# Two transformer blocks on one core: the tile scheduler orders the program by its timeline simulation instead of its default machine

## The chip, the cores and the metric

The kernel runs on one core of one Trainium2 chip. The metric is device time in microseconds of one execution, the median of several. The engines of the core are TensorE (PE; its weight loads have a row of their own, PEld), VectorE (DVE), ScalarE (ACT), GpSimd (POOL) and SyncE (SP), whose queue issues the DMA transfers.

## What is computed

The reference runs two blocks one after the other on 512 tokens of width 1024, all in float32:

```python
x = first_block(x, c, ctx, c_ctx, ...)      # 2 layers, modulated by c and c_ctx
return second_block(x, even_w_in_2, ...)    # 2 layers, each a mixer and a feed-forward
```

The first block normalises and modulates the tokens and 256 context tokens. Its layer 0 is windowed attention with 16 query heads, 4 key heads and a sink; the tokens also read all context keys. Its layer 1 is latent attention (16 heads, keys of 64 + 32) over context and tokens. Each layer ends with a gated output projection that is added to the tokens, and the block with a norm.

The second block has an even layer, in which 8 attention heads stand beside 4 heads of a linear recurrence (HGRN2, in blocks of 32 tokens), and an odd layer with 16 heads of chunked attention and a table of relative biases. After each mixer follow a norm, a residual sum, and a feed-forward of width 2816 with a convolution of three taps over the tokens, a GELU gate and a projection back.

## The kernel before, in words

**Arithmetic.** Large products are made of three TensorE products of fp32r halves: a weight tile is split into a high part H and a low part L, the activations too, and H·H, H·L and L·H are summed in PSUM (`gemm_T`, `oproj_chunk`). `mm` (L293) records every product, so nearly all matmuls carry its line, and `act` (L290) every ScalarE operation. `wchunk` (L295) brings one weight tile: a DMA into `raw` (L300), a ScalarE copy to H and a VectorE subtraction for L (L304). There are two or three buffers of `raw` and three of H and L.

**Stages, in the order of the trace.** Modulation and the turning of x (until about 100 us); attention of layer 0 (`attn_a`, until about 410); its output projection, gates and norms (`out_proj`, until about 500); the latent projections and gates of layer 1 and its attention (`attn_b`, until about 810); the output projection; the even mixer (`even`, about 880 to 1060); its output projection and norm (`mixer_end`); the feed-forward (`ffn`, until about 1470); the odd mixer (`odd`, until about 1700), `mixer_end` and the second feed-forward.

**Order in the program.** The kernel is written with Python generators. In attention `merge` and `mix` take turns between the scores of one head, the values of the head before, and filling work: the projections for coming heads (`g_qk`, `g_q`, `g_v`, `g_g`). `skew` makes the transposes of a block of P run two or three blocks ahead of the products that use them. Q and K of a pair of heads are gathered by DMA copies (`dcopy`, L591) from the projected tiles. There are 8 pairs in `attn_a`, 8 in `attn_b`, 4 in `even` and 8 in `odd`. In `out_proj` each row block's projection is followed by its residual sum and norm: `row_r` (L352, VectorE), `rstd` (L336, GpSimd, a power of -0.5), the product x·rstd (L365 or L367, VectorE, tile xhat), and then the transposes on TensorE (L375), which `turn` records some chunks of the next block's projection later. In `attn_b` the same is done with L1157 for the latent projections. In the recurrence of `even` (`g_h`) the tile U is made by TensorE and ScalarE, run through 14 dependent VectorE operations (L1556), used in products (po from U and hq), normalised, and transposed (L1582).

**What sets the order on the engines.** All operations are recorded inside one `TileContext`. When it is left, its scheduler runs the recorded program against a model of the machine: whenever an engine of the model can take an instruction, it is given the one of highest priority among those whose operands and buffers are ready in the model. Priority is the order of recording, shifted at L329 and L1738 by `high_priority(50)`; at L1567 `issue_after` ties the order of some products by hand. The sequence that each engine received in the model is the sequence of its queue on the chip, where each queue runs in order and waits by semaphores. The DMA queue of SyncE is ordered in the same way. The model before is the scheduler's default one.

## Time and profile before

| | |
|---|---|
| time, median of 3 runs | 2116.98 us (2109.93 to 2120.24) |
| profiled execution, its own time | 2119.62 us |
| its span, first to last instruction | 2117.8 us |
| instructions in the span | 28799, of which 10609 matmuls and as many weight loads |
| mean granted TensorE clock | 0.988 of full speed |
| moved by DMA | 223.65 MB, mean 106 GB/s |

Busy time of an engine is the time in which it has an instruction under way. Matmuls are pipelined, so the records of two of them overlap. "Idle before" is the time for which an engine stood still ahead of an instruction; the name behind the arrow is what ended it. [...]

### The profile page before, as it was taken

What the parts mean: (1) busy time and instruction counts of PE and PEld (TensorE: products, weight loads), DVE (VectorE), ACT (ScalarE), POOL (GpSimd) and SP (SyncE); (2) the same over time, 40 slices, a digit from 0 to 9 for tenths busy, and PEclk for the clock granted to TensorE, in tenths of its full rate; (3) what the DMA queues carried; (4) which work ended last, traced back from release to release, by engine and by line L of the source; (5) the groups of instructions that cost most, each with busy time, mean ns of one, the idle gap of its engine ahead of it and who ended that gap; (6) DMA issues with size and microseconds to landing.
All of it is one profiled execution on the core that took longest, in us unless ns stands there. A gap on an engine that the chain in (4) does not pass through costs nothing.

```text
span 2117.8 us, 28799 instructions
## 1 busy us (share of the span) xinstructions
PE 2032.1 (96%) x10609; PEld 1688.5 (80%) x10609; DVE 1293.2 (61%) x2491; ACT 1056.4 (50%) x2044; POOL 74.0 (3%) x162
## 2 busy tenths in 40 slices
PE   7899999998999999998999999999999999999998
PEld 4788888778788887876778888887888878888886
DVE  5588788846478886657756444423566775444323
ACT  5477677725367763555534333322466754333321
POOL 2100000000000000000000000000000000000000
PEclk9999999999999999999999999999999999999999
DMA  7344423322444332232223233232565533333332
GB/s 261 100 132 135 115 85 97 118 71 69 124 94 109 86 97 80 94 90 61 60 90 114 96 100 100 91 99 80 138 158 152 140 120 100 100 100 94 96 96 83
DMA packets 80893, 223.65 MB, mean 106 GB/s; under 512 B 13408, under 2 KB 19312, under 8 KB 80752
## 3 DMA queue, kind: packets, MB, share of 16 engines
q1 hardware_dynamic: 80752, 221.81, 34.8%
q8 instruction: 84, 1.38, 0.3%
q14 instruction: 57, 0.47, 0.1%
HBM read 176.67 MB, written 4.19 MB: 85 GB/s over the span
## 4 chain that ended last, share of the span: by engine, by line
PE 82%; DVE 7%; ACT 5%; issue 2%; DMA 2%; POOL 2%; SPq 0%; POOLq 0%; ACTq 0%; DVEq 0%
PE pj L293 33%; PE S L293 28%; PE po L293 13%; PE tp L293 2%; DVE wL L304 2%; PE tp L1305 2%; PE tp L1100 1%; ACT wH L290 1%; POOL rstd L336 1%; ACT tmp L290 1%; ACT junk L290 1%; DVE XL L584 1%; PE tp L375 1%; PE tp L1792 1%; ACT P L290 1%
## 5 line engine op out<-in xcount | busy, mean ns | idle before, releaser
L304 DVE TENSOR_TENSOR wL<-raw,wH 128x1024 fp32r<-128x1024 f32 (+2 forms) x291 | 354.1, 1221 | 465.4 <-ACT wH L290 453.2
L290 ACT ACTIVATE wH<-raw 128x1024 fp32r<-128x1024 f32 (+2 forms) x291 | 305.5, 1053 | 546.4 <-PE S L293 217.6
L293 PE MATMUL pj<-XH,wH 128*128 128x512 f32 (+1 forms) x672 | 259.9, 390 | 2.9 <-ACT tmp L290 1.5
L293 PE MATMUL pj<-XL,wH 128*128 128x512 f32 (+1 forms) x672 | 258.9, 389 | 0.1
L293 PE MATMUL pj<-XH,wL 128*128 128x512 f32 (+1 forms) x672 | 256.0, 384 | 0.5 <-DVE wL L304 0.5
L293 PE MATMUL S<-K,Q 96*128 96x384 f32 (+4 forms) x864 | 189.2, 329 | 3.9 <-ACT P L290 3.0
L293 PE MATMUL S<-XH,wH 128*128 128x512 f32 (+1 forms) x456 | 170.0, 373 | 1.0 <-ACT wH L290 1.0
L293 PE MATMUL S<-XH,wL 128*128 128x512 f32 (+1 forms) x456 | 170.1, 373 | 0.5 <-DVE wL L304 0.5
L293 PE MATMUL S<-XL,wH 128*128 128x512 f32 (+1 forms) x456 | 169.9, 373 | 0.0
L293 PEld LDWEIGHTS S<-K,Q 128*128 128x128 f32 (+1 forms) x864 | 140.7, 189 | 19.2 <-ACT P L290 7.3
L293 PEld LDWEIGHTS pj<-XH,wH 128*128 128x128 f32 x672 | 127.4, 190 | 28.5 <-ACT tmp L290 2.3
L293 PEld LDWEIGHTS pj<-XH,wL 128*128 128x128 f32 x672 | 127.0, 190 | 22.4 <-DVE wL L304 0.8
L293 PEld LDWEIGHTS pj<-XL,wH 128*128 128x128 f32 x672 | 127.1, 190 | 22.0 <-issue 0.4
L290 ACT ACTIVATE PTH<-tp 128x512 fp32r<-128x512 f32 (+2 forms) x192 | 91.3, 480 | 45.1 <-PE tp L1100 14.0
L584 DVE TENSOR_TENSOR PTL<-tp,PTH 128x512 fp32r<-128x512 f32 (+2 forms) x192 | 103.6, 543 | 10.2 <-ACT PTH L290 9.5
L293 PEld LDWEIGHTS S<-XH,wH 128*128 128x128 f32 x456 | 86.2, 189 | 16.6 <-ACT wH L290 1.7
L293 PEld LDWEIGHTS S<-XH,wL 128*128 128x128 f32 x456 | 86.2, 189 | 15.7 <-DVE wL L304 1.0
L293 PEld LDWEIGHTS S<-XL,wH 128*128 128x128 f32 x456 | 86.2, 189 | 15.2
L290 ACT ACTIVATE XH<-tp 128x512 fp32r<-128x512 f32 x128 | 75.1, 596 | 43.4 <-PE tp L375 24.0
L584 DVE TENSOR_TENSOR XL<-tp,XH 128x512 fp32r<-128x512 f32 x128 | 86.9, 686 | 10.6 <-ACT XH L290 9.5
L290 ACT ACTIVATE P<-S,nm 128x768 f32<-128x768 f32 (+1 forms) x96 | 72.5, 757 | 31.5 <-DVE nm L1018 12.4
L293 PE MATMUL po<-PTH,V 128*128 128x256 f32 (+1 forms) x224 | 78.8, 355 | 2.7 <-ACT PTH L290 2.3
(482 smaller groups left out, 4500.8 us busy)
## 6 DMA issues: line engine op xcount, KB each, us to landing
raw<-in_up SPq DMA_DIRECT2D x88, 512.0 KB, 3.5
raw<-in_ada SPq DMA_DIRECT2D x48, 512.0 KB, 4.2
raw<-in_dn SPq DMA_DIRECT2D x44, 512.0 KB, 3.5
raw<-in_o_o SPq DMA_DIRECT2D x11, 512.0 KB, 4.3
x<-in_x SPq DMA_DIRECT2D x8, 512.0 KB, 9.0
raw<-in_a_q SPq DMA_DIRECT2D x8, 512.0 KB, 4.7
raw<-in_a_g SPq DMA_DIRECT2D x8, 512.0 KB, 3.7
raw<-in_a_o SPq DMA_DIRECT2D x8, 512.0 KB, 3.6
```

Of the source, the lines that this page charges most:

```text
L290: self.nc.scalar.activation(out, in_, func, **kw)
L293: return self.nc.tensor.matmul(out, l, r, start=start, stop=stop, **kw)
L304: nc.vector.tensor_sub(L[:, :n], raw[:, :n], H[:, :n].bitcast(F32))
L336: self.nc.gpsimd.tensor_tensor(r, ms, self.c_mh[:, :n], op=ALU.pow)
L375: nc.tensor.transpose(tp[:, kk, :], xh[g][:, kk * P:(kk + 1) * P], self.ident)
L584: self.nc.vector.tensor_sub(L, src, H.bitcast(F32))
L1100: nc.tensor.transpose(tp[:, (i - i0) * P:(i - i0 + 1) * P], Ps[i][0][:, at(i) * P:(at(i) + 1) * P], self.ident)
L1305: nc.tensor.transpose(tp[:, i * P:(i + 1) * P], Ps[i][:, kb * P:(kb + 1) * P], self.ident)
L1792: nc.tensor.transpose(tp[:, (i - kb) * P:(i - kb + 1) * P], Ps[i][0][:, kb * P:(kb + 1) * P], self.ident)
```

## The change

The context is built with one more argument, by which its scheduler runs the program against its timeline simulation, a second model of the same machine with other durations and queues, in place of the default one. The recorded operations, their priorities, the buffers and the edges of `issue_after` are the same. Of the model's result only the order of each engine's queue, the order of the DMA queue and the choice among a tag's buffers go into the program.

```diff
-    with tile.TileContext(nc) as tc:
+    with tile.TileContext(nc, schedule_with_timeline_sim=True) as tc:
         Prog(tc, I, out).build()
```

## Rows read from the trace of the kernel before

**Rows 1.** The page, busy us, share of the span and instructions.
```profile
PE 2032.1 (96%) x10609; PEld 1688.5 (80%) x10609; DVE 1293.2 (61%) x2491; ACT 1056.4 (50%) x2044; POOL 74.0 (3%) x162
```
**Rows 2.** The page, the chain that ended last, by engine.
```profile
PE 82%; DVE 7%; ACT 5%; issue 2%; DMA 2%; POOL 2%; SPq 0%; POOLq 0%; ACTq 0%; DVEq 0%
```
**Rows 3.** Busy time by stretch; its first line says the columns.
```profile
core 0: us, PE busy (x) PEld busy (x) DVE busy (x) ACT busy (x) POOL busy (x), PEclk, DMA share, GB/s
0.00:100.00 100.00, 79.49 (x400) 60.37 (x401) 55.58 (x109) 46.25 (x95) 22.94 (x33) 0.95 0.56 187
100.00:400.00 300.00, 295.63 (x1778) 254.74 (x1776) 249.16 (x605) 219.61 (x465) 14.03 (x58) 1.00 0.35 103
400.00:600.00 200.00, 186.32 (x869) 153.93 (x870) 120.56 (x238) 89.33 (x191) 7.19 (x12) 0.95 0.34 107
600.00:800.00 200.00, 195.15 (x1157) 164.25 (x1156) 171.66 (x264) 139.50 (x277) 0.00 (x0) 1.00 0.37 96
...
900.00:1100.00 200.00, 181.81 (x1082) 146.01 (x1082) 125.75 (x287) 103.98 (x234) 4.60 (x5) 0.97 0.26 80
...
1150.00:1470.00 320.00, 320.00 (x1400) 262.75 (x1399) 133.62 (x154) 105.09 (x133) 0.15 (x1) 1.00 0.31 99
...
1530.00:1680.00 150.00, 147.06 (x875) 127.27 (x873) 104.46 (x325) 98.77 (x233) 2.32 (x12) 0.99 0.58 151
...
1790.00:2110.00 320.00, 320.00 (x1399) 262.44 (x1398) 128.05 (x150) 99.10 (x126) 1.65 (x3) 1.00 0.29 94
```
**Rows 4.** The chain in order of time, feed-forward: start us, us, what.
```profile
1187.81 5.44 PE pj L293 x24
```
**Rows 5.** TensorE by line and shape: count, busy us, mean ns, idle before.
```profile
L375 PE MATMUL tp<-ident,xhat 128*128 128x128 f32 x176 | 27.5, 287 | 13.6 <-DVE xhat L365 11.2 <-DVE modv L389 2.3
...
L293 PE MATMUL S<-i,kn 32*128 32x128 f32 x128 | 10.9, 285 | 3.6 <-ACT U L290 3.3 <-ACT kn L290 0.3
...
L1582 PE MATMUL tp<-ident,tmp 128*128 128x128 f32 x16 | 5.1, 327 | 5.6 <-DVE tmp L1577 5.6
...
L293 PE MATMUL po<-U,hq 128*32 128x128 f32 x120 | 4.3, 276 | 2.6 <-DVE U L1556 2.6
...
L1157 PE MATMUL tp<-ident,xhc 128*128 128x128 f32 x14 | 3.4, 292 | 3.2 <-DVE xhc L1144 2.0 <-DVE ss L1139 1.2
```
**Rows 6.** Timeline of TensorE, 838 to 848: start us, us, instruction, idle before.
```profile
838.66 0.39 PE L293 MATMUL pj<-wH,oH 128*128 128x512 f32 x1
840.13 0.66 PE L375 MATMUL tp<-ident,xhat 128*128 128x128 f32 x4 [1.08 <-DVE xhat L365]
840.54 0.48 PE L293 MATMUL pj<-wL,oH 128*128 128x512 f32 x1
```
**Rows 7.** Timeline of TensorE in the recurrence, 948 to 975.
```profile
956.35 0.39 PE L293 MATMUL pj<-XH,wL 128*128 128x512 f32 x1
959.32 1.07 PE L293 MATMUL po<-U,hq 128*32 128x128 f32 x30 [2.58 <-DVE U L1556]
963.32 0.47 PE L1582 MATMUL tp<-ident,tmp 128*128 128x128 f32 x1 [2.92 <-DVE tmp L1577]
```
**Rows 8.** Waits of SyncE's queue: us in total, times, longest us.
```profile
SPq L300 <- DVE wL L304: 1003.4, 199, 21.3
```
**Rows 9.** The page, the costliest group: all weight splits on VectorE.
```profile
L304 DVE TENSOR_TENSOR wL<-raw,wH 128x1024 fp32r<-128x1024 f32 (+2 forms) x291 | 354.1, 1221 | 465.4 <-ACT wH L290 453.2
```
**Rows 10.** Timeline of SyncE's queue in the odd mixer: the last copies of two pairs.
```profile
1585.20 1.24 SPq L591 DMA_DIRECT2D K<-tL  x2
...
1683.40 1.25 SPq L591 DMA_DIRECT2D K<-tL  x2
```
**Rows 11.** DMA issues: count, KB each, median us from issue to landing.
```profile
K<-tL SPq DMA_DIRECT2D x32, 128.0 KB, 2.3
```
**Rows 12.** Timeline of TensorE in the odd mixer: first scores of two heads.
```profile
1594.88 0.34 PE L293 MATMUL S<-K,Q 128*128 128x128 f32 x2
...
1687.97 0.30 PE L293 MATMUL S<-K,Q 128*128 128x128 f32 x1 [0.24 <-DMA K<-tL]
```

## The prediction

> **What bounds the kernel now.** I read the page's busy line first, then the chain of work that ended last, then the busy time by stretch, and last what the matmul queue waits for. TensorE is busy 2032.1 of 2117.8 us; VectorE stands at 61% and ScalarE at 50% [rows 1], and the chain runs through matmuls for 82% of its length [rows 2]. So the kernel is bound by the matmul queue, and a new order of the same instructions can only take from, or add to, the 85.7 us in which that queue stands idle, plus what the clock loses with it.
>
> The table by stretch says where those 85.7 us lie [rows 3]. The two feed-forward parts (1150 to 1470 and 1790 to 2110) are full to the last digit: 320.00 of 320. There the chain shows 24 matmuls in 5.44 us, one every 0.227 us [rows 4]. No order makes these 640 us shorter. The attention parts are nearly full: 4.4 us idle of 300 (100 to 400), 4.9 of 200 (600 to 800), 2.9 of 150 (1530 to 1680). The idle time sits elsewhere: 20.5 us in the first 100, 13.7 in 400 to 600 (end of the first mixer, start of the second), 18.2 in 900 to 1100 (the even mixer with its recurrence). In these three the granted clock is below one as well: 0.95, 0.95 and 0.97.
>
> **Part 1: transposes that stand too early in the queue.** The change alters no instruction, only the estimate by which the scheduler decides when an operand will be ready, and so who comes first on each engine. The trace shows where the present estimate is wrong. On TensorE 13.6 us are spent before the transposes of the normalised rows (L375) and 3.2 us before those of L1157; the recurrence adds 5.6 us (L1582), 2.6 (the product with U) and 3.6 (the product that makes U) [rows 5]. Sum: 28.6 us, a third of all idle time. One case in full [rows 6]: the output projection runs until 838.66, the queue then waits 1.08 us for VectorE's xhat, does four transposes at 840.13, and goes on with the very same projection at 840.54 (pj from wL and oH). The trace gives that projection no wait of its own; it only stood behind. The scheduler thought the chain VectorE, GpSimd, VectorE to be over about 1.1 us sooner than it is. An order that puts five projection matmuls (5 x 0.227 = 1.13 us) ahead of the transposes loses nothing.
>
> What is late next: ScalarE and VectorE split the transposed rows 1.1 us later, which matters only for the last row block of a stage, behind which there is no projection left. With four to six blocks per stage I count one in four of these waits as staying. The term is (13.6 + 3.2) x 3/4 = 12.6 us, its bounds 0 (the new estimate is as wrong as the old one) and 16.8.
>
> For the recurrence the case is less clean. At 956.35 the last ready matmul goes out, the product with U waits 2.58 us, the next transposes 2.92 us [rows 7], and only then a projection of 24 matmuls starts. If that projection's weights were there, it could have filled both holes; whether they were, the trace does not say. I take half of 5.6 + 2.6 + 3.6 = 11.8, which is 5.9 us; bounds 0 and 11.8.
>
> **Part 2: new holes in the attention parts.** These stages hold their two chains (scores of one head, values of the one before) closely interleaved, and another estimate will cut them elsewhere. The trace of before has no row for it, so I bound it: below zero by nothing, since their idle share is already the smallest outside the feed-forward; above by the worst stretch with the same kind of work, 900 to 1100, idle 9.1%. I take the poorest attention stretch, 600 to 800 (2.4% idle), for all of them: 300 us x 2.4% is 7.3 instead of 4.4, and 150 us x 2.4% is 3.7 instead of 2.9, together +3.7 us. At 9.1% the three stretches (650 us, 12.2 us idle now) would cost +47 us.
>
> **Part 3: the feed-forward parts, the start and the end.** Cost nothing. In the feed-forward, what hides a changed order is the prefetch of weights: VectorE is busy 133.6 us of 320 and ScalarE 105.1 [rows 3], so a weight tile split somewhat later still arrives in time. If that cover went, each of the two parts would pay for the missing weight tile in its first matmuls only. The first 100 us (granted clock 0.95, 20.5 us idle) and the last 8 us are chains that begin with the first load and end with the last store, with no other work at hand; I leave them as they are.
>
> [...]
>
> **The sum.** 12.6 + 5.9 - 3.7 = 14.8 us less. The profiled execution took 2119.62 us (span 2117.8 and 1.8 around it), 2.64 above the median of 2116.98; 2119.62 - 14.8 - 2.64 gives 2102 us, 0.7% faster.
>
> **The rivals.** *Nothing nets out (same).* The new order moves some waits later and makes others earlier. For it: the holes are spread over dozens of places, and what Part 1 gives is eaten by Part 2 as soon as the attention parts go from 2.4% to about 4.5% idle (650 us x 4.5% = 29 against 12.2). Against it: the waits in rows 5 are all of one sign. To this belongs the case that the switch changes hardly anything, because both estimates rank the ready instructions alike. Time: 2117 us.
>
> *Head copies behind weight loads (slower).* All transfers go out from SyncE's one queue in order, and this queue already stands 1003.4 us behind weight loads that wait for a buffer to come free, 199 times, 5.04 us each, 21.3 at most [rows 8]. There are 291 weight tiles [rows 9], so 68% of them wait. The copies that make Q and K of a pair of heads share this queue. If the new estimate puts a weight load ahead of a pair's copies, they go out 5.04 us later. What they can bear differs: for one pair the last copy is issued at 1585.20 and takes 1.24 us for two issues [rows 10], lands 2.3 us later [rows 11], and scores follow at 1594.88 [rows 12], a lead of 6.1 us; for another the last is issued at 1683.40 [rows 10], and the scores at 1687.97 already wait 0.24 us for it [rows 12]: no lead. At a mean lead of 3.1 us each hit costs 1.9 us; 28 pairs (8 + 8 + 4 + 8) x 0.68 x 1.9 = 36 us: 2153 us. It decides from the point where a load waits longer than the lead. For it: the copies have no slack in at least one place. Against it: in the trace of before nearly nothing on TensorE waits for them.
>
> *A much larger gain.* The order could let TensorE overlap weight loading and streaming better everywhere. In rows, the weight loads are busy 80% [rows 1], at best 254.74 of 300 us [rows 3]; all of the kernel at that share would take 1688.5 / 0.849 = 1989 us. Against it: in the feed-forward the share is only 262.75 of 320, 82%, and yet there is no idle time, so the share follows the width of the matmuls and not the order. [...]
>
> **How the numbers follow.** The forecast, waits shortened by more than new ones are made, has 0.43; the large gain 0.02; so faster by over 0.5% (about what a measurement of this kernel can tell from no change, 10.6 us) has 0.45. Nothing nets out: 0.25. Slower, by the copies or by attention parts at up to 9.1% idle (2117 + 47 = 2164): 0.30. The low end is the gain's far bound: 28.6 us of waits and 16 of clock off the median give 2072; I go to 2068. The high end, 2158, takes in the copies' 2153 and most of the way to 2164. The forecast's own range is 2072 to 2106.
>
> **What would show it.** In the profile after: the same counts, 10609 matmuls and 291 weight tiles; the idle time before L375 down from 13.6 to some 5 us, and projection matmuls standing before the transposes at the end of each stage; the stretch of the recurrence less than 18 us idle; both feed-forward parts still 320 of 320, each only begun earlier. If the waits at L375 are as long as before, Part 1 is wrong. If TensorE waits for DMA into K or Q, the copies were the thing. If attention stretches show over 4.5% idle, Part 2 was too small.

## The result and the profile after

The changed kernel takes 2187.11 us (median of four runs, 2185.10 to 2195.54), the kernel before 2118.05 on the same chip: ratio 1.0341, interval 1.0301 to 1.0381. It is slower by 69 us, where 15 us less were forecast, and it lies above the range that the prediction gave. The profiled execution has a span of 2193.7 us, 75.9 more than before, at a mean granted clock of 0.968 instead of 0.988.

The page's busy line of the changed kernel, to be held against [rows 1]:

```profile
PE 2054.3 (94%) x10609; PEld 1716.4 (78%) x10609; DVE 1288.9 (59%) x2491; ACT 1057.5 (48%) x2046; POOL 77.0 (4%) x162
```

The counts are the same, 10609 matmuls. TensorE's idle time rose from 85.7 to 139.4 us (+53.7) and its busy time by 22.2 us, though it does the same work. The second figure goes with the granted clock: in the second feed-forward part, at 1.00 in both kernels, 1399 matmuls take 320.00 us in each. Busy time by stretch says where both lie. The columns are those of [rows 3]; the bounds are the beginning and end of a part in this trace, or two points up to which TensorE has run the same matmuls in both kernels:

```profile
84.00:439.00 355.00, 325.03 (x1914) 279.98 (x1913) 267.11 (x649) 236.63 (x497) 15.89 (x58) 0.96 0.33 96
504.60:573.90 69.30, 68.08 (x377) 60.57 (x375) 49.27 (x120) 40.55 (x98) 5.39 (x9) 1.00 0.36 120
626.30:806.90 180.60, 172.29 (x1023) 146.47 (x1024) 153.57 (x236) 122.42 (x245) 0.00 (x0) 1.00 0.36 89
940.90:1118.70 177.80, 140.40 (x846) 114.31 (x845) 102.18 (x255) 81.74 (x202) 4.04 (x4) 0.84 0.18 54
1210.00:1530.00 320.00, 320.00 (x1401) 262.75 (x1400) 130.22 (x149) 102.88 (x128) 0.00 (x0) 1.00 0.29 97
1593.00:1784.00 191.00, 181.84 (x1047) 158.16 (x1046) 130.47 (x405) 120.82 (x287) 2.03 (x14) 0.97 0.54 142
1865.00:2185.00 320.00, 320.00 (x1399) 262.41 (x1398) 128.37 (x151) 99.25 (x126) 1.65 (x3) 1.00 0.28 94
```

The same stretches of the kernel before. The counts of matmuls agree within two, but for the odd mixer, the last line, which has 27 fewer here:

```profile
89.00:410.00 321.00, 315.54 (x1913) 272.19 (x1912) 266.79 (x648) 234.39 (x496) 14.03 (x58) 1.00 0.35 101
480.20:560.60 80.40, 73.91 (x375) 64.57 (x373) 48.83 (x120) 38.93 (x94) 5.30 (x9) 0.94 0.31 103
606.70:782.90 176.20, 172.71 (x1024) 146.36 (x1022) 152.67 (x237) 123.56 (x246) 0.00 (x0) 1.00 0.39 101
916.00:1057.50 141.50, 126.80 (x845) 102.11 (x845) 100.40 (x257) 83.52 (x203) 4.04 (x4) 0.95 0.23 68
1527.00:1703.00 176.00, 172.42 (x1020) 147.50 (x1018) 127.01 (x401) 117.77 (x281) 2.61 (x14) 0.99 0.56 147
```

The first attention part lasts 34 us longer: its idle time went from 5.5 to 30.0 us, and its busy time rose by 9.5 at a clock of 0.96 instead of 1.00. The even mixer lasts 36 us longer: 37.4 us idle instead of 14.7, and 13.6 more busy at a clock of 0.84 instead of 0.95. The odd mixer is 15 us longer (3.6 to 9.2 us idle). The second attention part loses 4 us (3.5 to 8.3 us idle). One stretch gained: the end of the first output projection with the latent projections behind it (the second line) takes 69.3 us instead of 80.4, with 1.2 us idle instead of 6.5 and a clock of 1.00 instead of 0.94. At the points with the same matmuls behind them, the changed kernel is late by 29.3 us after the first attention part, by 13.3 after that gain, by 23.9 at the end of the second attention part, by 25.0 at the start of the even mixer's line and 61.2 at its end, by 63.6 through the first feed-forward and by 75.6 through the second. The feed-forward parts are what they were, 320.00 of 320.

Which waits these are, TensorE's table of waits tells (waited for, us in total, times, longest):

```profile
PE po L293 <- DVE U L1556: 13.7, 4, 6.0
PE tp L375 <- DVE xhat L365: 7.4, 3, 3.8
PE S L293 <- DMA Q<-tL: 7.3, 4, 3.1
PE tp L1100 <- DVE PTL L584: 7.1, 10, 1.9
...
PE pj L293 <- ACT hq L290: 5.2, 3, 3.1
...
PE pj L293 <- DVE sgx L942: 3.8, 4, 1.8
...
PE S L293 <- DMA K<-tH: 3.5, 3, 1.4
...
PE S L293 <- DMA K<-tL: 2.2, 2, 1.2
```

No single wait carries the 54 us; the longest kind, the product with U, rose by 11.1 [rows 5]. That hole is the one of [rows 7]. TensorE's timeline of the kernel before, ahead of those rows, and then that of the changed kernel show how it grew:

```profile
945.60 1.15 PE L293 MATMUL S<-i,kn 32*128 32x128 f32 x10 [0.41 <-ACT U L290]
...
950.28 1.20 PE L293 MATMUL po<-i,sT 128*128 128x128 f32 x8
```
```profile
980.41 0.39 PE L293 MATMUL pj<-XH,wL 128*128 128x512 f32 x1
...
982.63 1.15 PE L293 MATMUL S<-i,kn 32*128 32x128 f32 x8 [0.19 <-ACT U L290]
...
985.69 1.16 PE L293 MATMUL po<-i,sT 128*128 128x128 f32 x8 [0.82 <-DVE sT L1550]
992.87 1.93 PE L293 MATMUL po<-U,hq 128*32 128x128 f32 x30 [6.03 <-DVE U L1556]
997.89 0.79 PE L293 MATMUL pj<-XH,wH 128*128 128x512 f32 x1 [3.08 <-ACT hq L290]
998.48 0.63 PE L293 MATMUL pj<-XL,wH 128*128 128x512 f32 x1
998.90 0.63 PE L293 MATMUL pj<-XH,wL 128*128 128x512 f32 x1
...
1001.89 0.40 PE L293 MATMUL pj<-XH,wH 128*128 128x512 f32 x1
1002.12 0.40 PE L293 MATMUL pj<-XL,wH 128*128 128x512 f32 x1
```

In the kernel before, the same `po<-i,sT` began at 950.28 and a projection ran behind it up to 956.35 [rows 7]; the wait for U was 2.58 us. Now the projection has been run ahead of it, until 980.41, and nothing is left to stand in the hole: 6.03 us, and 3.08 more behind it. U itself came no later: from the last `S<-i,kn` to its product with hq it took 13.7 us before (945.60 to 959.32) and takes 10.2 now (982.63 to 992.87). The matmuls that follow come 0.42 us apart (998.48 to 998.90), at a granted clock of 0.50 (998.00 to 1001.00), and 0.23 us apart from 1001.89 on, at 1.00 (1002.00 to 1004.00). So this place loses twice: the two waits, 9.11 us together, and the nine matmuls from 997.89 to 1001.89, which take 4.00 us where nine at 0.23 us would take 2.07. No run below changes the even mixer alone, so its 36 us are read from the two traces only.

### The profile page after: what moved, and what is told of

It reads as the page before. It is cut to its first block, busy times and chain, and to the rows that moved or that the text cites. A ratio compares the mean times of both kernels' runs of the same rounds, so it can differ in the third digit from the quotient of the medians.

```text
span 2193.7 us, 28900 instructions
## 1 busy us (share of the span) xinstructions
PE 2054.3 (94%) x10609; PEld 1716.4 (78%) x10609; DVE 1288.9 (59%) x2491; ACT 1057.5 (48%) x2046; POOL 77.0 (4%) x162
## 5 line engine op out<-in xcount | busy, mean ns | idle before, releaser
L293 PE MATMUL pj<-XH,wH 128*128 128x512 f32 (+1 forms) x672 | 267.1, 399 | 16.3 <-ACT hq L290 5.2
L293 PE MATMUL pj<-XL,wH 128*128 128x512 f32 (+1 forms) x672 | 265.5, 396 | 5.6 <-DVE XL L584 5.4
L293 PE MATMUL pj<-XH,wL 128*128 128x512 f32 (+1 forms) x672 | 264.8, 395 | 0.0
L293 PEld LDWEIGHTS pj<-XH,wH 128*128 128x128 f32 x672 | 133.2, 198 | 44.7 <-ACT hq L290 6.3
L293 PEld LDWEIGHTS pj<-XL,wH 128*128 128x128 f32 x672 | 133.0, 198 | 30.4 <-DVE XL L584 7.1
L293 PEld LDWEIGHTS pj<-XH,wL 128*128 128x128 f32 x672 | 132.6, 197 | 24.2 <-issue 0.2
L290 ACT ACTIVATE XH<-tp 128x512 fp32r<-128x512 f32 x128 | 74.4, 595 | 43.9 <-PE tp L375 24.5
```

The lines of the kernel that those rows point to most:

```text
L290: self.nc.scalar.activation(out, in_, func, **kw)
L293: return self.nc.tensor.matmul(out, l, r, start=start, stop=stop, **kw)
```

## The experiments

All kernels below record the same operations. To hold a queue to an order, the recorded order of one kernel is added as a chain of dependencies between neighbours of that queue, which put no wait into the program:

```diff
-    with tile.TileContext(nc) as tc:
+    with tile.TileContext(nc, schedule_with_timeline_sim=True) as tc:
         Prog(tc, I, out).build()
+        keep_order(tc)        # for each queue held: add_manual_dep(next, previous, NoSync)
```

The runs differ in which queues are listed, in whose order, and in the flag of the first line.

**One queue at a time: TensorE back to before, all but TensorE back, TensorE alone to after, SyncE back.**

```diff
+ held to before: PE                 (e1_pe, timeline simulation)
+ held to before: SP, ACT, DVE, POOL (e2_others, timeline simulation)
+ held to after:  PE                 (e3_default_pe, default machine)
+ held to before: SP                 (e4_sp, timeline simulation)
```

> Timeline machine as in the changed kernel, but the order of TensorE's queue is held to that of the kernel before; the other queues are free. Theory A (TensorE's queue: work is brought forward in it and missing later): back to 2118 us, within 10. Theory B (the DMA queue: copies of Q and K stand behind weight loads): the queue of SyncE is still the new machine's, so most of the loss stays, 2160 or more. Theory C (the in-order queues of ScalarE and VectorE): between, 2140 to 2180.

> The reverse: timeline machine with the orders of SyncE, ScalarE, VectorE and GpSimd held to those of the kernel before, TensorE's queue free. Theory A: most of the loss stays, 2160 or more (less if TensorE's order follows the others back). Theory B and C: back to about 2118 us.

> Default machine, with TensorE's order held to that of the changed kernel; other queues free. Theory A: 2187 us, within 15, the loss without the new machine. Theory B or C: 2118 to 2140.

> Timeline machine, with only the order of SyncE's DMA queue held to that of the kernel before. Theory B: back to 2118 to 2135 us, and TensorE no longer waits for DMA into Q or K. Theory A or C: 2175 to 2190, as the changed kernel.

Measured, as ratios to the kernel before: 1.0380 (1.0359 to 1.0400), 1.0968 (1.0942 to 1.0994), 1.050 (2220.93 us, one run) and 1.046 (2213.31 us, one run). The first result surprised most: TensorE's matmuls stand exactly as before, 10609 of them, and the kernel still takes 2193.61 us. The second shows that the reverse is worse still: the old order of the four feeders (the queues of SyncE, ScalarE, VectorE and GpSimd), with TensorE's queue free, costs 198 us of span. TensorE's order there is a third one, about 9 places on average from each of the two kernels' (the n-th instruction of a kind in one trace against the n-th in the other). None of the three theories has all four numbers right. So no one queue carries the loss by itself, and an order taken from one kernel does not fit another's. Whether the order was the cause at all, or the buffers that the scheduler deals out along with it, stood open.

**Everything held, and one feeder free.** TensorE and all but one feeder are held to before, under the timeline simulation.

```diff
+ held to before: PE, DVE, ACT, SP, POOL (e5_all)
+ held to before: PE, DVE, ACT           (e7_pad)
+ held to before: PE, DVE, SP, POOL      (e8_act_free)
+ held to before: PE, ACT, SP, POOL      (e9_dve_free)
```

> Timeline simulation on, and all five queues held to the order of the kernel before; what is still free is the choice of buffers and with it the waits. Theory A (the order of the queues is the whole of it): the time of the kernel before, 2118 us, within 0.5%. Rival B (the timeline simulation also deals out buffers so that instructions wait for other ones): 2140 to 2190 us although the order is the same.

> Timeline simulation on, TensorE, ScalarE and VectorE held to the order of the kernel before, SyncE and GpSimd free. With TensorE alone held the time was 2193.6 us. Theory C (the loss comes from the feeders' small moves, ScalarE and VectorE most of all): below 2130 us. Rival D (the loss left there sits in SyncE's queue, weight loads and head copies): about 2160 to 2190 us, with waits of TensorE for the DMA into K, Q or for the weights' splits.

> Timeline simulation on, all queues but ScalarE's held to the order of the kernel before. ScalarE's order then differs from before's by 0.3 places on average. Theory C with ScalarE as the carrier: 2150 to 2190 us. If VectorE or SyncE is the carrier: below 2130 us. If no one queue matters by itself and only moves in several of them add up: 2118 to 2135 us here and in the run with VectorE free.

> Timeline simulation on, all queues but VectorE's held to the order of the kernel before. VectorE's order then differs from before's by 0.7 places on average. Theory C with VectorE as the carrier: 2150 to 2190 us. If ScalarE or SyncE is the carrier: below 2130 us. If only moves in several queues add up: 2118 to 2135 us here and in the run with ScalarE free.

Measured: 2118.34 us (1.0022, 1.0005 to 1.0038), 2121.87 (1.0035, 1.0020 to 1.0050), 2159.07 (1.0216, 1.0135 to 1.0297) and 2155.34 (1.0198, 1.0130 to 1.0267). Theory A holds: with the order fixed, the switch changes nothing that matters. Against the run with all queues held, ScalarE's freedom costs 40.7 us, VectorE's 37.0, SyncE's and GpSimd's together 3.5, which is within the spread of the runs; the sum, 81, is near the 75.3 us by which the run with TensorE alone held lies above it. SyncE's queue, on which my slower rival rested, is thus almost without effect as long as TensorE's order is the old one.

With the same order on TensorE, one place can be followed in both traces. (`PTH` and `PTL` are the high and the low half of a transposed block of P, `po` is the accumulator of a head's values, `OC` their sum for the context tokens, `OT` that for the tokens, `l` a row sum.) First ScalarE's and then TensorE's timeline around one head of the first attention part, with every queue held:

```profile
193.00 0.57 ACT L290 ACTIVATE PTH<-tp 128x512 fp32r<-128x512 f32 x1
194.06 0.60 ACT L290 ACTIVATE PTH<-tp 128x512 fp32r<-128x512 f32 x1 [0.49 <-PE tp L1100]
...
195.49 0.38 ACT L290 ACTIVATE tmp<-po 64x256 f32<-64x256 f32 x1
195.77 1.05 ACT L290 ACTIVATE wH<-raw 128x1024 fp32r<-128x1024 f32 x1
```
```profile
196.32 0.38 PE L1100 MATMUL tp<-ident,P 128*128 128x128 f32 x2
196.63 0.49 PE L293 MATMUL po<-PTH,V 128*128 128x512 f32 x1
```

The same with ScalarE's order free:

```profile
201.75 0.71 ACT L290 ACTIVATE P<-P,l 128x512 f32<-128x512 f32 x1
203.68 1.06 ACT L290 ACTIVATE wH<-raw 128x1024 fp32r<-128x1024 f32 x1 [1.22 <-DMA raw<-in_a_k]
204.65 0.58 ACT L290 ACTIVATE PTH<-tp 128x512 fp32r<-128x512 f32 x1
205.12 1.05 ACT L290 ACTIVATE wH<-raw 128x1024 fp32r<-128x1024 f32 x1
...
207.00 0.38 ACT L290 ACTIVATE tmp<-po 64x256 f32<-64x256 f32 x1
```
```profile
203.08 0.28 PE L293 MATMUL po<-PTL,V 128*128 128x256 f32 x1
...
205.19 0.38 PE L1100 MATMUL tp<-ident,P 128*128 128x128 f32 x2
208.14 0.50 PE L293 MATMUL po<-PTH,V 128*128 128x512 f32 x1 [2.58 <-DVE OC L608]
```
```profile
207.01 0.16 DVE L1069 RECIPROCAL l<-l 128x1 f32<-128x1 f32 x1 [1.06 <-ACT P L290]
...
207.68 0.41 DVE L608 TENSOR_TENSOR OC<-po,tmp 64x256 f32<-64x256 f32 x1
```

Two weight splits now stand ahead of the copy `tmp<-po`. The first one makes ScalarE wait 1.22 us for a load that has not landed, and each takes 1.05 us. The copy comes 2.35 us behind the last `PTH` here, 1.43 behind it before. VectorE's sum OC (L608) needs the copy; ahead of it in VectorE's queue stands L1069, which waits 1.06 us for a row sum that ScalarE also makes behind the splits. The sum ends TensorE's wait for the accumulator po, and TensorE stands for 2.58 us where it had not stood at all. In the held order both splits stand behind the copy, the first at 195.77. ScalarE kept to the order of its queue here: the product that the copy reads ended at 203.36 us (203.08 and 0.28), and the copy still came behind both splits, at 207.00. Such waits for OC sum to 5.8 us in this part; a larger kind, of the products of P and V for PTH, sums to 10.9 us, and the table of the run with every queue held lists neither here. That gave two theories: on ScalarE the weight splits that were put ahead, on VectorE the maxima and masks of a later head put ahead of the low half that TensorE needs next.

**One-sided rules.** Only one kind of move is forbidden; everything else in the free queue stays free. A rule is a set of the same dependencies, from the 40 instructions ahead (or to the 40 behind) in the old order.

```diff
+ e8_act_free + wH not ahead of its old place                (e10_act_w)
+ e9_dve_free + nothing may pass PTL, tL                     (e11_dve_low)
+ after       + wH, wL not ahead, nothing may pass PTL, tL   (e12_both)
+ before, second attention part in the order of after        (e13_hyb)
```

> As the run with ScalarE alone free (2159 us, 41 us over the run with every queue held), but the high halves of the weight splits (wH, 291 on ScalarE) may not pass what stands ahead of them in the order of the kernel before; the rest of ScalarE's queue stays free. Theory M1 (weight splits put ahead of the softmax's exponentials and copies carry ScalarE's loss): below 2130 us, and TensorE reaches the end of the first attention part within 5 us of the kernel before, where it was 23 us late. Rival (the other small moves carry it): 2145 us or more.

> As the run with VectorE alone free (2155 us, 37 us over the run with every queue held), but the low halves that TensorE takes next (PTL, tL) may not be passed by what stands behind them in the order of the kernel before; the rest of VectorE's queue stays free. Theory M2 (maxima and masks of a later head put ahead of the low half that TensorE waits for carry VectorE's loss): below 2130 us. Rival (other moves carry it): 2145 us or more.

> The changed kernel, all queues free under the timeline simulation, with only these one-sided rules: no half of a weight split (wH on ScalarE, wL on VectorE) earlier than in the order before, no low half (PTL, tL) passed by what stood behind it. Theory (the feeders' order is the cause, TensorE's own new order costs nothing): below 2140 us. Rival (TensorE's new order costs too): 2160 to 2190 us, against 2187 without the rules.

> Default machine, every queue held to the order before except in the second attention part, where all queues hold the order of the changed kernel, which gained 8.5 us there. If gain and loss of a part are its own: 2105 to 2113 us, faster than both kernels. If the gain only paid back a delay that came from the parts ahead: 2116 to 2125 us.

Measured: 1.0057 (1.0041 to 1.0074), 1.0195 (1.0174 to 1.0215), 1.0449 (1.0429 to 1.0470), 1.0022 (1.0005 to 1.0038).

The first theory holds, if only just (2129.33 us against "below 2130", 5.8 against "within 5"): one rule for 291 instructions gives back three quarters of ScalarE's loss, 2159.07 to 2129.33 us, and the first attention part ends 5.8 us late instead of 23.1. In that part the waits for OC fall from 5.8 to 0.9 us, those for PTH only from 10.9 to 7.9. The second fell. The waits at which it aimed did go: the transposes' waits for PTL, 5.2 us at L1792 and 4.4 at L1100, are no longer among the largest. But others came in their place, as the table of TensorE's waits of that run shows, and the time stayed:

```profile
PE po L293 <- DVE U L1556: 7.6, 3, 3.7
...
PE po L293 <- ACT PTH L290: 4.9, 7, 2.6
```

With the low halves' rule and the order of all else free, the U of the recurrence came later (3.6 us of waits without the rule). The third run says that the rules do not rescue the changed kernel: it became slower, 2212.83 us. TensorE's order was free in it and moved too, by about 8 places on average from the changed kernel's, so it does not price the rules alone; TensorE's own new order had to be tried apart from them. The fourth was to beat both kernels, and it did not. Its expectation rests on a gain of 8.5 us in the second attention part, which the traces do not show when the same matmuls are compared: there the changed kernel loses, and its gain lies ahead, in the projections. The run, in which the first stretch has the new order for its larger part, repeats both in small; the lines are to be held against those of 480.20 and 606.70 above:

```profile
478.60:554.00 75.40, 71.29 (x374) 63.41 (x373) 48.32 (x118) 39.19 (x95) 5.35 (x9) 0.95 0.34 110
604.30:784.40 180.10, 172.21 (x1023) 146.37 (x1024) 153.70 (x236) 122.40 (x245) 0.00 (x0) 1.00 0.36 90
```

The first stretch is 5.0 us shorter than before, the second 3.9 longer. In the run with every queue held, whose order is that of the kernel before, the same two differ from it by 1.3 and 0.2 us. A kernel with the new order in the first stretch alone was not run.

**VectorE's moves apart, and TensorE's main move alone.** Pairing the two orders of TensorE's queue, projections of the first attention part stand some 20 to 45 places earlier in the changed kernel, by kind, and transposes and products of P and V 45 to 49 later.

```diff
+ e9_dve_free + wL not ahead of its old place             (e14_dve_w)
+ e9_dve_free + P, nm, nmt not ahead of their old places  (e15_dve_max)
+ before      + projections ahead of softmax, as in after (e16_proj)
```

> As the run with VectorE alone free (2155 us, 37 us over the run with every queue held), but the low halves of the weight splits (wL, 291) may not pass what stands ahead of them in the order before. If VectorE loses the way ScalarE does (by weight splits put ahead of softmax work): below 2130 us. If its loss lies in the order of the softmax work itself: 2140 us or more.

> As the run with VectorE alone free, but the masks, maxima and their copies (P, nm, nmt) may not pass what stands ahead of them in the order before. Theory (work of a later head put ahead of what TensorE needs for the present one, be it a low half, a V, a row sum or a U): below 2130 us, with TensorE's waits for PTL and V near those of the run with every queue held. Rival (many kinds of moves, no one of which carries it): 2140 us or more.

> Default machine, all queues free, with one rule: in the first and the last attention part a projection's matmul stands ahead of the same transposes and PV matmuls as in the changed kernel. The other queues adapt to that under the default machine. Theory F (projections are the filler for the softmax's waits; spent early they are missing later): 2140 to 2200 us, the loss in those two parts and none in the second attention part. Rival (TensorE's order is free as long as the feeders' order fits it): 2112 to 2128 us.

Measured: 2136.44 us (1.0096, 1.0060 to 1.0132), 2140.52 (1.0117, 1.0066 to 1.0169) and 2164.39 (1.0230, 1.0196 to 1.0264). On VectorE both kinds carry a part: the weight splits give back 19 of the 37 us, masks and maxima 15. The first time lies between the two numbers named, the second, from two runs, at the 2140 of the rival by which no one kind carries the loss. TensorE's move costs 2.3% with the other queues following it under the default machine, in which ScalarE's and VectorE's orders move by about 2 places on average, so it isn't free. The loss sits in the first attention part alone (47 us at its end, 44 at the end of the kernel); in the odd mixer, where it was expected too, the same rule cost nothing. TensorE's lines of that part (idle time behind the second bar, with what ended it) show the projections themselves waiting, because they now stand ahead of what makes their operands and frees their accumulators:

```profile
L293 PE MATMUL pj<-XH,wH 128*128 128x512 f32 x128 | 53.8, 420 | 12.6 <-DVE sgc L942 7.0 <-ACT wH L290 5.6
...
L1100 PE MATMUL tp<-ident,P 128*128 128x128 f32 x256 | 43.1, 279 | 3.4 <-DVE PTL L584 3.1
```

In the kernel before, the first of these groups waits 0.9 us in that stretch and the second 1.0. So theory F is right in the sign and in one of its two places, but half of the mechanism is another: most of the 16 us shown, of 35.4 us idle in that stretch, are not fillers missing later but projections that came too early.

**Do the parts add up?** TensorE held, all feeders free, with the rules that gave something back.

```diff
+ e1_pe + wH, wL not ahead                   (e17_pe_w)
+ e1_pe + wH, wL, P, nm, nmt not ahead       (e18_pe_w_max)
```

> As the run with TensorE alone held to the order before (2193.6 us, 75 us over the run with every queue held), but neither half of a weight split (wH on ScalarE, wL on VectorE) may pass what stands ahead of it in the order before. With one queue free at a time this rule gave back 30 us on ScalarE and 19 us on VectorE. If these add up when all feeders are free: 2140 to 2150 us. Rival (free together, the feeders lose by other moves, as the changed kernel did under its rules): 2170 us or more.

> As the run before it, and the masks, maxima and their copies (P, nm, nmt) on VectorE may not pass what stands ahead of them either, which gave back 15 us with VectorE alone free. If the parts add up: 2125 to 2135 us. Rival: 2160 us or more.

Measured: 2162.90 us (1.0212, 1.0173 to 1.0251) and 2151.10 (1.0156, 1.0125 to 1.0187), from 2193.61. The two rules for weight splits give back 31 us where 49 were the sum, the third 12 where 15 were; both runs lie between the two cases. Of the 75 us some 43 have names; 33 us are spread over moves that I did not take apart. These are the 75 us of the run with TensorE held. In the changed kernel TensorE's order differs from before's by 15 places on average, ScalarE's by 3.5 and VectorE's by 4.5 (0.3 for ScalarE in the run in which it alone is free). That the orders make its 69 us is shown; how the 69 us divide over its moves is not.

## Why the prediction was wrong

**What bounds the kernel** was right, and so was the statement that an order can only add to or take from TensorE's idle time, plus what the clock loses. The two gave +53.7 and +22.2 us.

**Part 1** had the right sign at half the size for the transposes, and the wrong sign for the recurrence. After, for [rows 5]:

```profile
L375 PE MATMUL tp<-ident,xhat 128*128 128x128 f32 x176 | 25.4, 281 | 9.8 <-DVE xhat L365 7.4 <-DVE XL L584 2.3
...
L293 PE MATMUL S<-i,kn 32*128 32x128 f32 x128 | 12.6, 288 | 2.7 <-ACT kn L290 2.5 <-ACT U L290 0.2
...
L293 PE MATMUL po<-U,hq 128*32 128x128 f32 x120 | 7.7, 420 | 13.7 <-DVE U L1556 13.7
...
L1582 PE MATMUL tp<-ident,tmp 128*128 128x128 f32 x16 | 3.5, 313 | 3.0 <-DVE tmp L1577 3.0
...
L1157 PE MATMUL tp<-ident,xhc 128*128 128x128 f32 x14 | 2.7, 271 | 0.0
```

L375 and L1157 went from 16.8 to 9.8 us, 7.0 less where 12.6 were forecast. The recurrence went from 11.8 to 19.4 where 5.9 were forecast. The five holes together are where they were, 28.6 before and 29.2 after. In one place the mechanism came as forecast, the clock with it: the stretch from 480.20 to 560.60, which holds the transposes of L1157, became 11.1 us shorter, 5.3 of them idle time and 5.8 busy time, at a clock of 1.00 instead of 0.94. The mistake in the recurrence is visible in the working: I asked whether a projection could be moved into the hole, and did not ask whether the one that already filled most of it might be moved out.

**Part 2 is the step that failed.** I let new holes cost 3.7 us: their "idle share is already the smallest outside the feed-forward", so I saw nothing to gain there, and took the poorest of these parts, 2.4%, as the likely value. Measured are 8.4% in the first (30.0 of 355), 4.6% in the second (8.3 of 180.6) and 4.8% in the odd mixer (9.2 of 191), so the bound of 9.1% was the better guess for the first, and the test that the prediction set itself, over 4.5%, is met in all three, in the second barely. Idle time rose by 34.9 us in the three together (24.5, 4.8 and 5.6). The even mixer had no term for new holes at all; its 22.7 us more idle are 7.6 in the recurrence, which the sum had as a gain of 5.9, and 15 in other waits. A small idle share is no sign that there is slack. Here it was a sign that the queues' orders fit each other, and the runs with one feeder free show how little it takes to spoil that: ScalarE alone, moved by 0.3 places on average, costs 1.9%. For a change that reorders every queue the bound should have been weighed as the likely value.

**The clock** was counted only as a possible gain of 16 us. It went the other way: 22 us more of busy time for the same matmuls, for which the sum had no term. The 16 us were my estimate, what the granted 0.95 and 0.97 lack of 1.00 over 200 us each, 10 and 6 [rows 3]; no run shows them as a gain, and in place of it the runs showed this loss and, in the one stretch that gained, 5.8 us less of busy time. The two stretches of the table with the most new idle time, 24.5 and 22.7 us, have the lowest clock, 0.96 and 0.84; whether the idle time alone lowered it was not shown.

**Part 3** was right for the feed-forward: 320.00 of 320, and the delay does not change within either part.

**The rivals.** The one with head copies behind weight loads showed in part. SyncE's waits for buffers rose from 1003.4 to 1133.7 us [rows 8], and TensorE's waits for DMA into K and Q rose from 0.2 us to 14.5 (7.3 + 3.5 + 2.2 and two of 0.9 and 0.6), not to 36. But SyncE's order is not the cause by itself: free together with GpSimd's it costs 3.5 us, and with the changed kernel's SyncE taken back to before, its one run was slower, 2213.31 us. Slower by the attention parts, at 2164 us, was the nearest case, and had no more than a part of 0.30. It lacked the clock and the even mixer, so its nearness to the measured time is in part chance.

## What to carry to other kernels

Where one engine is 96% busy and several in-order queues feed it, as here, the order of the queues is one object: one feeder's order, changed by less than a place on average, cost 2%, and the feeders of one kernel under another order of TensorE cost nearly 10%. Price a change of the scheduler's estimate by what the tightest parts can lose, not by the waits that are visible now. And to find a cause in such a change, hold all queues to the old order and free one at a time; then forbid one kind of move.

## What the runs showed of the hardware that was not expected

The price of a ScalarE instruction in the wrong place was not its duration. A cast of a weight tile took 1.05 us; two of them ahead of a 0.38 us copy, with 1.22 us of waiting for a load, made TensorE idle for 2.58 us, and the rule against moves of this kind gave back 30 us. And the even mixer lost more than the length of its new holes: it had a granted clock of 0.84 in the changed kernel, with matmuls 0.42 us apart behind a hole, at 0.50, and 0.23 us further on, at 1.00, and of the 36 us that it lost 13.6 were busy time.
